# Feed-forward combinations joined to 1024 columns, and the scale of the up values on ScalarE

## The chip, the cores and the metric

The kernel runs on one core of a Trainium2 chip. The metric is the device time of one execution in microseconds (us), the median of three runs. Five engines work in parallel, each through its own list of instructions in a fixed order: TensorE (PE, with its weight loads shown apart as PEld), VectorE (DVE), ScalarE (ACT), GpSimd (POOL) and SyncE (SP), which issues most of the transfers. An instruction that has to wait holds back all that stands behind it on its engine.

## The reference

Two layers work on 256 positions of 2048 features in float32. Each layer is a mixer (first a gated delta rule beside a linear recurrence, then two kinds of attention) and a feed-forward part. Only the feed-forward part is touched here:

```python
def swiglu(hn, w_gate, w_up, w_down):
    return (jax.nn.silu(hn @ w_gate) * (hn @ w_up)) @ w_down
...
        h = h + swiglu(rmsnorm(h, ffn_norm[layer]), ffn_w_gate[layer], ffn_w_up[layer], ffn_w_down[layer])
    return rmsnorm(h, final_norm)
```

The inner width is 5632. `h` is the residual. The factor 1/rms of the norm is not applied to the input of the products but to their results, one number for each position (`nrm["rs"]`).

## The kernel before

**Products in three parts.** A float32 product is made of three products of a shorter float type. Each weight tile `raw` (128 partitions x 1024 columns) is loaded by SP, rounded by ACT to `whi` (L179), and the rest `wlo = raw - whi` is made by DVE (L180). PE then does high x high, high x low and low x high (L409, L410, L411), 512 columns each. Four buffers hold `whi`, three hold `wlo`. So each weight tile costs one ACT and one DVE instruction of 1024 columns before PE can use it.

**Blocks.** In `ffn` the work comes in blocks. A gate block makes 512 columns of the gate product and 512 of the up product for two groups of 128 positions; a down block makes 1024 columns of the down product. A block sums in four PSUM banks `F[t][i]`: `t` is the group of positions and `i` gate or up (in a down block, the left or right half). There are 11 gate blocks and 6 down blocks in each of the two feed-forward parts, in three pieces of 4, 4 and 3 gate blocks, each with two down blocks behind it. All blocks but the first of each part take a share of their weights in Strassen's way, with seven products in place of eight: sums of weight tiles (`T`, L384, split into `thi` at L376 and `tlo` at L377) meet combinations of the inputs (`comb`, made in `combine`, L387 to L398), and the results go into four more banks `M[0]` to `M[3]`. The `acc` pool has four banks for `F`, the `msp` pool four for `M` and for the transposes.

**The sums over the banks.** When its seven products are done, `ends` (L460) joins the banks `M` into four tiles of 128x512 in SBUF, `e[t][i]`: an ACT copy of `M[0]` and four DVE additions or subtractions (L464), each with one bank as input. After the block a gate block adds `F` to each tile (L529 for gate, L533 for up), takes the SiLU of the gate on ACT with the scale by 1/rms (L530), and multiplies: one DVE `scalar_tensor_tensor` for each `t` that scales the up values and multiplies them by the gate (L534). A down block adds `h` to each of the four tiles (L554), and then the sum to `F`, which gives the new `h` (L561; L557 at the very end).

**What follows.** The result of a gate block is transposed by PE into two banks `Ph` (`turn`, L498) in the next block, copied by ACT (L507), and its low part is taken by DVE (L508). These are the inputs `hid` of the down blocks.

**The order.** The program is written in the order of the algorithm; a planner that works with costs of its own puts the instructions of each engine into their final order. Only the end of the last block on DVE and ACT is ordered by hand. Where an instruction becomes shorter or waits for something else, the planner can put its neighbours elsewhere too, on every engine.

Of the kernel before, what the change touches and what calls it, by code (L numbers as in the profile page):

```python
# [5 lines left out]
AF = mybir.ActivationFunctionType  # L6
# [41 lines left out]
def body(tc, A, out):  # L48
# [338 lines left out]
    def combine(x4):  # L387
# [6 lines left out]
        for i, (x, y) in enumerate(((a21, a22), (a21, a11), (a22, c[:, 1]), (a12, c[:, 2]))):  # L394
            V.tensor_tensor(out=c[:, i], in0=x, in1=y, op=ALU.subtract)
# [18 lines left out]
    def sums():  # L414

        return [[mx.tile([128, 512], F32, name=f"e{t}{i}", tag=f"e{t}{i}", bufs=1) for i in range(2)] for t in range(2)]

    def block(src, x, comb, nd, hooks, tail=0, lead=2, trail=None):
# [41 lines left out]
        def ends():  # L460
            (c1, w5), (v, w7) = sums()
            S.copy(c1, M[0].t)
            for o, a, b, op in ((v, M[2], c1, ALU.subtract), (w5, M[1], v, ALU.add), (v, M[3], v, ALU.add), (w7, M[3], w5, ALU.add)):
                V.tensor_tensor(out=o, in0=a.t, in1=b, op=op)  # L464
            return [[c1, w5], [v, w7]]
# [27 lines left out]
    def ffn(L, then, fin=None):  # L493
# [18 lines left out]
        for groups in ((0, 2, 2, 2), (2, 2, 2, 2), (2, 2, 2)):  # L512
            piece = len(groups)
            hid = ogp.tile([128, 16, 2, T], F32R, name="hid", tag="hid")
            late = {4: lambda hid=hid: ch.update({0: combine(hid[:, 0:4])})}
            for j in range(piece):
                hooks = {2: turn} if todo else {}
                if b == 0:
                    hooks[5] = lambda: cx.update({0: combine(X[:, 0:4])})
                    hooks[8] = rstd  # L520
                    hooks[10] = lambda: cx.update({1: combine(X[:, 4:8])})
                if j == 1 and piece == 3:

                    hooks[6] = late[4]
                F, e = block(lambda i, u: gu[b, u, i], lambda k: X[:, k], {m: lambda m=m: cx[m] for m in range(groups[j])}, 4, hooks)
                a = e or sums()
                for t in range(2):
                    if e:
                        V.tensor_tensor(out=a[t][0], in0=F[t][0], in1=e[t][0], op=(ALU.add, ALU.subtract)[t])  # L529
                    S.activation(a[t][0], a[t][0] if e else F[t][0], AF.Silu, scale=nrm["rs"][:, t:t + 1])  # L530
                for t in range(2):
                    if e:
                        V.tensor_tensor(out=a[t][1], in0=F[t][1], in1=e[t][1], op=ALU.add)  # L533
                    V.scalar_tensor_tensor(out=a[t][0], in0=a[t][1] if e else F[t][1], scalar=nrm["rs"][:, t:t + 1],  # L534
                                           in1=a[t][0], op0=ALU.mult, op1=ALU.mult)
                    todo.append((hid, j, t, a[t][0]))
                b += 1
            u0 = 2 * (b - piece)
            for p in range(2):
                end = b == NB and p == 1  # L540
                hooks = {2: turn} if todo else {}
                if p == 0 and piece == 4:
                    hooks.update(late)
# [754 lines left out]
```

## Time and profile before

| what | value |
|---|---|
| median of three runs | 2227.28 us (2226.58 to 2227.33) |
| the profiled execution's own time | 2228.4 us |
| its span | 2226.6 us |
| busy share of the span | PE 99%, PEld 83%, DVE 86%, ACT 58%, POOL 2% |
| mean granted clock of TensorE | 0.999 |
| first feed-forward part (first to last of its products) | 432.4 to 1127.9 us |
| second feed-forward part | 1524.5 to 2217.7 us |

In the rows of the profile, `out<-in` names the tiles, `xN` is a count, and what follows the bar is the busy time, the mean of one instruction in ns, and the idle time of the engine before them with what ended it. In the time-ordered view the first number is the start, the second the length. On DVE and ACT the recorded lengths of neighbours overlap by a little, so what one more instruction costs is read from start to start.

### The profile page before, as it was taken

The page shows a single profiled execution, that of the slowest core. Times are in us where ns is not written, and L with a number is a line of the kernel's source. Part 1 is how long each engine was busy: PE and PEld are TensorE (multiplying, and loading weights), DVE is VectorE, ACT ScalarE, POOL GpSimd, SP SyncE. Part 2 cuts the span into 40 slices and gives each one's busy share as a digit, 9 for nine tenths or more (in the row PEclk, how much of TensorE's full clock was granted, in tenths as well). Part 3 has the DMA queues.
Part 4 walks back from the last instruction along what each step waited for, and adds up shares of the span by engine and source line. Part 5 has one row for each costly group of instructions (what it writes and reads, how often), then busy time and mean ns, then how long its engine had stood idle before and what let it go on. Part 6 is the DMA issues. An engine that isn't in the chain of part 4 may idle for free.

```text
span 2226.6 us, 30372 instructions
## 1 busy us (share of the span) xinstructions
PE 2211.8 (99%) x11002; PEld 1847.0 (83%) x11002; DVE 1917.1 (86%) x2713; ACT 1284.9 (58%) x1687; POOL 50.6 (2%) x62
## 2 busy tenths in 40 slices
PE   9999999999999999999999999999999999999998
PEld 8888888888888888888878888888888888888886
DVE  8899676679999999999966658866999999999998
ACT  6776664555555665555654444545665566555565
POOL 0000000000000000000000000000000000000000
PEclk9999999999999999999999999999999999999999
DMA  7445445677777776777665455556777777777774
GB/s 281 155 146 163 141 152 184 208 223 227 212 227 231 220 233 211 225 230 225 193 196 171 161 169 175 168 178 185 223 226 216 221 225 238 219 214 239 218 236 151
DMA packets 125992, 451.67 MB, mean 203 GB/s; under 512 B 14065, under 2 KB 15601, under 8 KB 125713
## 3 DMA queue, kind: packets, MB, share of 16 engines
q1 hardware_dynamic: 117488, 420.10, 58.3%
q0 software_dynamic: 8064, 29.36, 7.8%
q8 instruction: 86, 1.41, 0.3%
q14 instruction: 66, 0.53, 0.1%
q10 hardware_dynamic: 288, 0.27, 0.0%
HBM read 447.58 MB, written 2.10 MB: 202 GB/s over the span
## 4 chain that ended last, share of the span: by engine, by line
PE 95%; DVE 2%; issue 1%; ACT 1%; DMA 1%; DVEq 0%; ACTq 0%
PE F L411 15%; PE F L410 15%; PE F L409 15%; PE Pw L199 10%; PE Pw L204 5%; PE Px L303 5%; PE Px L304 5%; PE Px L305 5%; PE M L410 5%; PE M L411 4%; PE M L409 4%; PE Ph L503 1%; DVE wlo L180 1%; PE Psc L1068 1%; PE Pt L326 0%
## 5 line engine op out<-in xcount | busy, mean ns | idle before, releaser
L179 ACT CAST whi<-raw 128x1024 fp32r<-128x1024 f32 x720 | 755.3, 1051 | 666.8 <-PE F L411 263.8
L180 DVE TENSOR_TENSOR wlo<-raw,whi 128x1024 fp32r<-128x1024 f32 x720 | 874.5, 1219 | 189.3 <-PE Px L304 70.1
L199 PE MATMUL Pw<-X,whi 128*128 128x512 f32 x1088 | 388.3, 400 | 0.0
L409 PE MATMUL F<-whi,X 128*128 128x512 f32 x848 | 331.4, 391 | 0.0
L410 PE MATMUL F<-wlo,X 128*128 128x512 f32 x848 | 330.4, 390 | 0.0
L411 PE MATMUL F<-whi,X 128*128 128x512 f32 x848 | 330.0, 389 | 0.0
L204 PE MATMUL Pw<-X,wlo 128*128 128x256 f32 x1088 | 304.8, 280 | 1.0 <-DVE wlo L180 0.9
L376 ACT CAST thi<-T 128x1024 fp32r<-128x1024 f32 x168 | 176.6, 1051 | 124.1 <-DVE T L384 84.0
L199 PEld LDWEIGHTS Pw<-X,whi 128*128 128x128 f32 x1088 | 204.2, 188 | 47.7 <-issue 0.5
L377 DVE TENSOR_TENSOR tlo<-T,thi 128x1024 fp32r<-128x1024 f32 x168 | 205.1, 1221 | 28.0 <-ACT thi L376 27.3
L204 PEld LDWEIGHTS Pw<-X,wlo 128*128 128x128 f32 x1088 | 205.3, 189 | 2.4 <-DVE wlo L180 2.0
L409 PE MATMUL F<-whi,hid 128*128 128x512 f32 x480 | 187.5, 391 | 0.0
L411 PE MATMUL F<-whi,hid 128*128 128x512 f32 x480 | 186.9, 389 | 0.0
L410 PE MATMUL F<-wlo,hid 128*128 128x512 f32 x480 | 186.8, 389 | 0.0
L411 PEld LDWEIGHTS F<-whi,X 128*128 128x128 f32 x848 | 159.2, 188 | 33.1
L409 PEld LDWEIGHTS F<-whi,X 128*128 128x128 f32 x848 | 159.2, 188 | 32.7
L410 PEld LDWEIGHTS F<-wlo,X 128*128 128x128 f32 x848 | 159.2, 188 | 32.4
L384 DVE TENSOR_TENSOR T<-T,raw 128x1024 f32<-128x1024 f32 x112 | 136.5, 1219 | 1.1 <-DMA raw<-in_gu 0.2
L410 PE MATMUL M<-tlo,comb 128*128 128x512 f32 x336 | 131.8, 392 | 1.1 <-DVE tlo L377 1.0
L409 PE MATMUL M<-thi,comb 128*128 128x512 f32 x336 | 131.4, 391 | 0.0
L411 PE MATMUL M<-thi,comb 128*128 128x512 f32 x336 | 130.9, 390 | 0.0
L411 PEld LDWEIGHTS F<-whi,hid 128*128 128x128 f32 x480 | 90.1, 188 | 18.8
(389 smaller groups left out, 3409.5 us busy)
## 6 DMA issues: line engine op xcount, KB each, us to landing
raw<-in_gu SPq DMA_DIRECT2D x352, 512.0 KB, 4.4
raw<-in_dn SPq DMA_DIRECT2D x176, 512.0 KB, 4.4
raw<-in_w0w SPq DMA_DIRECT2D x72, 512.0 KB, 3.6
raw<-in_wo SPq DMA_DIRECT2D x64, 512.0 KB, 3.6
raw<-in_w1w SPq DMA_DIRECT2D x64, 512.0 KB, 3.6
raw<-in_gu POOLq DMA_DIRECT2D x40, 512.0 KB, 6.8
raw<-in_w1x SPq DMA_DIRECT2D x32, 512.0 KB, 3.7
raw<-in_w0x SPq DMA_DIRECT2D x16, 512.0 KB, 3.6
```

The source lines that it names most:

```text
L179: S.copy(hi, raw)
L180: V.tensor_sub(lo, raw, hi.bitcast(F32))
L199: PE.matmul(P.rearrange("p a b -> p (a b)"), hi[:, kk], X[:, k].rearrange("p a b -> p (a b)"), start=k == 0, stop=False)
L204: PE.matmul(P[:, 0], lo[:, kk], X[:, k, 0], start=False, stop=k == NK - 1)
L303: PE.matmul(Ps[t], x[:, 0, ts], hi[:, kk], start=k == 0, stop=False)
L304: PE.matmul(Ps[t], x[:, 0, ts], lo[:, kk], start=False, stop=False)
L376: S.copy(hi, t)
L377: V.tensor_sub(lo, t, hi.bitcast(F32))
L384: V.tensor_tensor(out=t, in0=a, in1=b, op=ALU.add)
L409: PE.matmul(self.t, xh, hi[:, kk], start=self.i == kk == 0, stop=False)
L410: PE.matmul(self.t, xh, lo[:, kk], start=False, stop=False)
L411: PE.matmul(self.t, xl, hi[:, kk], start=False, stop=kk == 1 and self.i == self.n - 1)
```

## The change

Four edits:

1. In `combine` two of the four combinations of the inputs change their sign: the second is a11 - a21 (it was a21 - a11), the third a21 - a22 - a11 (it was the negative of that). The third is made from the first and no longer from the second. The count and the size of the instructions stay.
2. The four tiles `e[t][i]` become one tile `e` of 128x4x512. With the two signs turned, `ends` needs two DVE instructions of 512 columns and one of 1024 columns, which reads the bank `M[1]` twice and writes both up columns. This one needs `M[3]` to be done, and it is the last to read `M[1]`.
3. In a gate block the four additions of `F` stay. The up values are scaled by an ACT instruction each (L533, `Copy` with a scale), and one DVE multiplication of 1024 columns (L534) takes the place of the two of L534 before. It waits for all four ACT instructions.
4. In a down block `h` is added in two DVE instructions of 1024 columns (L553) and no longer in four of 512. The four additions of `F` (L561, L557) stay.

Two lambdas for the combinations of `hid` are also joined to one function, which moves nothing by itself. The line numbers of the changed kernel are used for it: L463, L464 and L465 are the three DVE instructions of `ends`, L532 is the addition of `F`.

```diff
-        for i, (x, y) in enumerate(((a21, a22), (a21, a11), (a22, c[:, 1]), (a12, c[:, 2]))):
-            V.tensor_tensor(out=c[:, i], in0=x, in1=y, op=ALU.subtract)
+        for i, x, y, op in ((0, a21, a22, ALU.subtract), (1, a11, a21, ALU.subtract), (2, c[:, 0], a11, ALU.subtract), (3, a12, c[:, 2], ALU.add)):
+            V.tensor_tensor(out=c[:, i], in0=x, in1=y, op=op)
...
-        return [[mx.tile([128, 512], F32, name=f"e{t}{i}", tag=f"e{t}{i}", bufs=1) for i in range(2)] for t in range(2)]
+        return mx.tile([128, 4, 512], F32, name="e", tag="e", bufs=1)
...
-            (c1, w5), (v, w7) = sums()
-            S.copy(c1, M[0].t)
-            for o, a, b, op in ((v, M[2], c1, ALU.subtract), (w5, M[1], v, ALU.add), (v, M[3], v, ALU.add), (w7, M[3], w5, ALU.add)):
-                V.tensor_tensor(out=o, in0=a.t, in1=b, op=op)
-            return [[c1, w5], [v, w7]]
+            e = sums()
+            S.copy(e[:, 0], M[0].t)
+            V.tensor_tensor(out=e[:, 1], in0=M[2].t, in1=e[:, 0], op=ALU.add)
+            V.tensor_tensor(out=e[:, 2], in0=M[3].t, in1=e[:, 1], op=ALU.add)
+            V.tensor_tensor(out=e[:, 1::2], in0=M[1].t.rearrange("p (a n) -> p a n", a=1).to_broadcast([128, 2, 512]),
+                            in1=e[:, 1:3], op=ALU.subtract)
+            return e
...
-                for t in range(2):
-                    if e:
-                        V.tensor_tensor(out=a[t][0], in0=F[t][0], in1=e[t][0], op=(ALU.add, ALU.subtract)[t])
-                    S.activation(a[t][0], a[t][0] if e else F[t][0], AF.Silu, scale=nrm["rs"][:, t:t + 1])
-                for t in range(2):
-                    if e:
-                        V.tensor_tensor(out=a[t][1], in0=F[t][1], in1=e[t][1], op=ALU.add)
-                    V.scalar_tensor_tensor(out=a[t][0], in0=a[t][1] if e else F[t][1], scalar=nrm["rs"][:, t:t + 1],
-                                           in1=a[t][0], op0=ALU.mult, op1=ALU.mult)
-                    todo.append((hid, j, t, a[t][0]))
+                for i, f in enumerate((AF.Silu, AF.Copy)):
+                    for t in range(2):
+                        if e is not None:
+                            V.tensor_tensor(out=a[:, 2 * t + i], in0=F[t][i], in1=a[:, 2 * t + i], op=ALU.add)
+                        S.activation(a[:, 2 * t + i], F[t][i] if e is None else a[:, 2 * t + i], f, scale=nrm["rs"][:, t:t + 1])
+                V.tensor_tensor(out=a[:, 0::2], in0=a[:, 1::2], in1=a[:, 0::2], op=ALU.mult)
+                for t in range(2):
+                    todo.append((hid, j, t, a[:, 2 * t]))
...
-                for t in range(2):
-                    for i in range(2):
-                        V.tensor_tensor(out=e[t][i], in0=hs[t][i], in1=e[t][i], op=ALU.subtract if t > i else ALU.add)
+                c = slice(2 * p * 512, (2 * p + 2) * 512)
+                for t in range(2):
+                    et = e[:, 2 * t:2 * t + 2].rearrange("p a n -> p (a n)")
+                    V.tensor_tensor(out=et, in0=h[:, t, c], in1=et, op=ALU.add)
```

Since the planner sets the order anew, instructions move. Three places matter to the prediction.

**DVE, from one gate block to the next** (the first Strassen block of the first part and the one behind it). `F` with its number is the old block's bank, `wlo<-raw_5347` in the first list and `wlo<-raw_5342` in the second belong to the new block's first weight tile, the `wlo` behind it to the second. Before:

```order
L180 TENSOR_TENSOR wlo<-raw,whi 128x1024
L529 TENSOR_TENSOR e_5250<-F_4972,e_5250 128x512
L384 TENSOR_TENSOR T<-T,raw 128x1024
L529 TENSOR_TENSOR e_5252<-F_4974,e_5252 128x512
L533 TENSOR_TENSOR e_5251<-F_4973,e_5251 128x512
L180 TENSOR_TENSOR wlo<-raw_5347,whi 128x1024
L534 SCALAR_TENSOR_TENSOR e_5250<-e_5251,rs,e_5250 128x512
L533 TENSOR_TENSOR e_5253<-F_4975,e_5253 128x512
L180 TENSOR_TENSOR wlo<-raw,whi 128x1024
L534 SCALAR_TENSOR_TENSOR e_5252<-e_5253,rs,e_5252 128x512
```

With the change:

```order
L180 TENSOR_TENSOR wlo<-raw,whi 128x1024
L532 TENSOR_TENSOR e<-F_4970,e 128x512
L180 TENSOR_TENSOR wlo<-raw_5342,whi 128x1024
L532 TENSOR_TENSOR e<-F_4972,e 128x512
L532 TENSOR_TENSOR e<-F_4971,e 128x512
L384 TENSOR_TENSOR T<-T,raw 128x1024
L532 TENSOR_TENSOR e<-F_4973,e 128x512
L180 TENSOR_TENSOR wlo<-raw,whi 128x1024 x2
L534 TENSOR_TENSOR e<-e 128x2x512
```

The second `wlo` of the new block stands behind the fourth addition of `F` in both lists. The sum of weights `T` has moved from before the second addition to just ahead of the fourth, and the multiplication, once two instructions among the `wlo`, now comes as one behind two of them.

**DVE, from a down block to the gate block behind it** (from the first piece to the second). `F_6378` and `F_6380` before, `F_6361` and `F_6363` with the change, are the banks that PE finishes last. Before:

```order
L554 TENSOR_TENSOR e_6644<-h,e_6644 128x512
L180 TENSOR_TENSOR wlo<-raw_6721,whi 128x1024
L561 TENSOR_TENSOR h<-F_6377,e_6641 128x512
L180 TENSOR_TENSOR wlo<-raw,whi 128x1024
L561 TENSOR_TENSOR h<-F_6379,e_6643 128x512
L561 TENSOR_TENSOR h<-F_6378,e_6642 128x512
L384 TENSOR_TENSOR T<-raw_6757,raw 128x1024
L561 TENSOR_TENSOR h<-F_6380,e_6644 128x512
L180 TENSOR_TENSOR wlo<-raw_6757,whi 128x1024
```

With the change:

```order
L465 TENSOR_TENSOR e<-M_6365,e 128x2x512
L377 TENSOR_TENSOR tlo<-T,thi 128x1024
L553 TENSOR_TENSOR e<-h,e 128x1024 x2
L561 TENSOR_TENSOR h<-F_6360,e 128x512
L561 TENSOR_TENSOR h<-F_6362,e 128x512
L561 TENSOR_TENSOR h<-F_6361,e 128x512
L180 TENSOR_TENSOR wlo<-raw_6698,whi 128x1024
L561 TENSOR_TENSOR h<-F_6363,e 128x512
L180 TENSOR_TENSOR wlo<-raw,whi 128x1024
```

The first `wlo` of the new gate block (`raw_6721` before, `raw_6698` now) has moved from ahead of the first addition of `F` to behind the third.

**PE, the same place.** The first products of the new gate block. Before:

```order
L409 MATMUL F_6713<-whi,X 128x512
L410 MATMUL F_6713<-wlo,X 128x512
L411 MATMUL F_6713<-whi,X 128x512
L409 MATMUL F_6713<-whi,X 128x512
L410 MATMUL F_6713<-wlo,X 128x512
```

With the change:

```order
L409 MATMUL F_6690<-whi,X 128x512
L409 MATMUL F_6692<-whi,X 128x512
L409 MATMUL F_6691<-whi,X 128x512
L409 MATMUL M_6694<-whi,X 128x512
L409 MATMUL M_6695<-thi,comb 128x512
L410 MATMUL F_6690<-wlo,X 128x512
```

Five products that need no low part are drawn ahead of the first that does. This happens at four places, at the first gate block of the second and third piece of each part. The same drawing ahead, by one or two products, stood at more places before, around `M[3]`.

More of the change, by code (lines that the diff above doesn't have):

```diff
@@ L514, in ffn @@
             hid = ogp.tile([128, 16, 2, T], F32R, name="hid", tag="hid")
-            late = {4: lambda hid=hid: ch.update({0: combine(hid[:, 0:4])})}
+            chs = lambda m, hid=hid: lambda: ch.update({m: combine(hid[:, 4 * m:4 * m + 4])})
             for j in range(piece):
@@ L542, in ffn @@
                 if p == 0 and piece == 4:
-                    hooks.update(late)
-                    hooks[9] = lambda hid=hid: ch.update({1: combine(hid[:, 4:8])})
+                    hooks.update({4: chs(0), 9: chs(1)})
                 if end and fin:
@@ L549, in ffn @@
                 F, e = block(lambda i, u: dn[2 * p + i, u0 + u], lambda k: hid[:, k],
-                             {m: lambda m=m: ch[m] for m in range(1 + (p == 1 and piece == 4))}, piece, hooks, *last)
+                             {m: lambda m=m: ch[m] for m in range(2 if p == 1 and piece == 4 else 1)}, piece, hooks, *last)
+                c = slice(2 * p * 512, (2 * p + 2) * 512)
+                for t in range(2):
+                    et = e[:, 2 * t:2 * t + 2].rearrange("p a n -> p (a n)")
+                    V.tensor_tensor(out=et, in0=h[:, t, c], in1=et, op=ALU.add)
                 hs = [[h[:, t, (2 * p + i) * 512:(2 * p + i + 1) * 512] for i in range(2)] for t in range(2)]
-                for t in range(2):
-                    for i in range(2):
-                        V.tensor_tensor(out=e[t][i], in0=hs[t][i], in1=e[t][i], op=ALU.subtract if t > i else ALU.add)
                 if end and fin:
                     with tc.manual_schedule(engines={V.engine, S.engine}):
-                        fin(lambda t, i: V.tensor_tensor(out=hs[t][i], in0=F[t][i], in1=e[t][i], op=ALU.add))
+                        fin(lambda t, i: V.tensor_tensor(out=hs[t][i], in0=F[t][i], in1=e[:, 2 * t + i], op=ALU.add))
                     continue
@@ L560, in ffn @@
                     for i in range(2):
-                        V.tensor_tensor(out=hs[t][i], in0=F[t][i], in1=e[t][i], op=ALU.add)
+                        V.tensor_tensor(out=hs[t][i], in0=F[t][i], in1=e[:, 2 * t + i], op=ALU.add)
                 if b == NB and not fin:
```

4 lines of the change are left out of this document (2 added, 2 removed).

## The prediction

> **What bounds the kernel now.** I read the page first, its busy line and its chain of waits:
>
> ```profile
> PE 2211.8 (99%) x11002; PEld 1847.0 (83%) x11002; DVE 1917.1 (86%) x2713; ACT 1284.9 (58%) x1687; POOL 50.6 (2%) x62
> PE 95%; DVE 2%; issue 1%; ACT 1%; DMA 1%; DVEq 0%; ACTq 0%
> ```
>
> PE is the chain, and DVE is the only other engine near its limit. The change touches the two feed-forward parts alone, so their stretches come next (columns: length, then busy time and count of PE, PEld, DVE, ACT, POOL, then clock, DMA share and GB/s):
>
> ```profile
> 432.40:1127.90 695.50, 694.66 (x3113) 573.15 (x3112) 652.97 (x698) 408.59 (x454) 24.32 (x28) 1.00 0.74 221
> 1524.50:2217.70 693.20, 692.89 (x3097) 571.44 (x3096) 646.90 (x691) 404.79 (x440) 24.17 (x28) 1.00 0.73 217
> 2217.70:2226.60 8.90, 0.18 (x1) 0.00 (x0) 4.11 (x10) 3.02 (x7) 0.00 (x0) 0.80 0.63 236
> ```
>
> A busy PE need not be a PE at full pace, since the products overlap. So I measure the pace from the starts. Between these two rows lie 56 steps of 512 columns each, none missing:
>
> ```profile
> 999.17 0.39 PE L410 MATMUL F<-wlo,X 128*128 128x512 f32 x1
> 1011.86 0.39 PE L409 MATMUL M<-thi,comb 128*128 128x512 f32 x1
> 2121.94 0.87 PE Ph L503 x8
> ```
>
> 12.69 / 56 = 0.2266 us for one product; a group of eight short transposes takes 0.87 us. The second part holds 3097 PE instructions, 96 of them short (88 of `Ph`, 8 of the norm): 3001 x 0.2266 + 12 x 0.87 = 690.4 us, of 693.2. The first holds 112 short ones: 680.0 + 14 x 0.87 = 692.2, of 695.5. So at full pace the two parts would be 2.8 + 3.3 = **6.1 us** shorter. That is the ceiling for anything that DVE or ACT can give back there. The waits by name say what part of it is real waiting (us in total, times, longest):
>
> ```profile
> PEld M L410 <- DVE tlo L377: 4.0, 8, 1.2
> PEld F L410 <- DVE tlo L377: 1.2, 6, 0.2
> ACT whi L179 <- PE F L411: 263.8, 217, 4.5
> ```
>
> 5.2 us in 14 places, all for a `tlo` of DVE. The rest is put down to no wait. The longest place:
>
> ```profile
> 968.62 0.39 PE L409 MATMUL F<-whi,X 128*128 128x512 f32 x1
> 969.77 0.50 PE L410 MATMUL M<-tlo,comb 128*128 128x512 f32 x1 [0.76 <-DVE tlo L377]
> 968.50 1.21 DVE L377 TENSOR_TENSOR tlo<-raw,thi 128x1024 fp32r<-128x1024 f32 x1
> ```
>
> PE has 969.77 - 968.62 - 0.23 = 0.9 us of waiting here, for a `tlo` that started at 968.50.
>
> **The change part by part.** The groups that it touches, and the 1024-column addition that stands for the new ones:
>
> ```profile
> L464 DVE TENSOR_TENSOR e<-M,e 128x512 f32<-128x512 f32 x128 | 84.9, 684 | 2.5 <-PE M L411 1.9
> L554 DVE TENSOR_TENSOR e<-h,e 128x512 f32<-128x512 f32 x48 | 31.2, 682 | 0.0
> L534 DVE SCALAR_TENSOR_TENSOR e<-e,rs,e 128x512 f32<-128x512 f32 x40 | 29.6, 745 | 0.0
> L384 DVE TENSOR_TENSOR T<-T,raw 128x1024 f32<-128x1024 f32 x112 | 136.5, 1219 | 1.1 <-DMA raw<-in_gu 0.2
> L530 ACT ACTIVATE e<-e,rs 128x512 f32<-128x512 f32 x40 | 28.5, 721 | 17.8 <-DVE e L529 17.1
> ```
>
> The recorded lengths overlap, so the price is read from start to start, in DVE's rows from a down block to the gate block behind it:
>
> ```profile
> 678.26 0.68 DVE L554 TENSOR_TENSOR e<-h,e 128x512 f32<-128x512 f32 x1
> 678.86 1.28 DVE L464 TENSOR_TENSOR e<-M,e 128x512 f32<-128x512 f32 x2
> 680.06 1.88 DVE L554 TENSOR_TENSOR e<-h,e 128x512 f32<-128x512 f32 x3
> 681.87 1.21 DVE L180 TENSOR_TENSOR wlo<-raw,whi 128x1024 fp32r<-128x1024 f32 x1
> 683.00 0.68 DVE L561 TENSOR_TENSOR h<-F,e 128x512 f32<-128x512 f32 x1
> 683.81 1.23 DVE L180 TENSOR_TENSOR wlo<-raw,whi 128x1024 fp32r<-128x1024 f32 x1
> 684.96 1.28 DVE L561 TENSOR_TENSOR h<-F,e 128x512 f32<-128x512 f32 x2
> 686.15 1.21 DVE L384 TENSOR_TENSOR T<-raw,raw 128x1024 f32<-128x1024 f32 x1
> ```
>
> 512 columns: (681.87 - 680.06) / 3 = 0.60 us. 1024 columns: 683.00 - 681.87 = 1.13 us. Joining two saves 1.20 - 1.13 = 0.07 us. The scaled multiplication is read at 519.24 and 519.90 in the fence below: 0.66 us.
>
> - `ends`, 32 blocks: 4 x 0.60 becomes 2 x 0.60 + 1.13, 32 x 0.07 = 2.2 us off DVE. The new operation reads one bank twice; no row shows that form. Its bounds are 1.13 (L384) and 1.20 us (two of L464); I take 1.13, since L464 and L554 cost alike with and without a bank.
> - The residual, 12 blocks: 12 x 2 x 0.07 = 1.7 us off.
> - The multiplication, 22 gate blocks: 2 x 0.66 becomes 1.13, 22 x 0.19 = 4.2 us off. The two blocks without Strassen's products are among them.
> - The signs in `combine`: as many instructions of the same size, no time.
> - ACT: 44 more instructions like L530, 44 x 0.72 = 31.7 us. ACT idles 286.9 + 288.4 = 575 us in the two parts, most of it because `whi` has no free buffer (the 263.8 us above). Cover enough; without it the price would be the 31.7.
> - Transfers: as many, of the same size.
>
> DVE: -8.1 us of 1300, 0.25 us a block. It lies beside PE, so it reaches the end only through the waits for `tlo`. By the 14 places, each shorter by no more than 0.25, that is 3.5 us at most, and nothing where the weights came late. I take **-1.0**, bounds 0 and -5.2.
>
> [...]
>
> **The waits that move.** First the down-to-gate places. PE's rows there:
>
> ```profile
> 684.92 0.39 PE L411 MATMUL F<-whi,hid 128*128 128x512 f32 x1
> 686.50 0.39 PE L409 MATMUL F<-whi,X 128*128 128x512 f32 x1
> ```
>
> The gate block begins at 686.50. Its first `wlo` was ready at 683.08 (681.87 + 1.21), 3.6 us ahead of its use. Now it stands behind the third addition of `F`. Laid on the same times: from 678.26 come `T` 1.13, 0.60, 1.13, `tlo` 1.13, 2 x 1.13 and two additions 1.20, which is 685.7; less the 0.6 that the first row of `ends` no longer takes ahead of it, 685.1. The third bank is done at 684.92 + 0.39 = 685.3. So the addition starts between 685.3 and 685.7, the `wlo` 0.60 later, and is ready between 687.1 and 687.5. PE, with five products drawn ahead, wants it at 686.50 + 5 x 0.227 = 687.6. It fits, by 0.1 to 0.5 us where it was 3.6. Bounds over the four places: 0 and 4 x 1.9 = 7.6 us (if it came behind the fourth addition as well, with its bank at 686.7 and 0.6 + 1.2 us behind that, and the next one late too). I take 4 x 0.1 = **+0.4**. A full bank is freed in time: the third by 686.3, PE wants it at 686.96.
>
> Second, the gate-to-gate places. The block of these rows begins at 518.66:
>
> ```profile
> 518.66 0.39 PE L409 MATMUL F<-whi,X 128*128 128x512 f32 x1
> 525.69 0.39 PE L410 MATMUL M<-tlo,comb 128*128 128x512 f32 x1
> 519.24 0.75 DVE L534 SCALAR_TENSOR_TENSOR e<-e,rs,e 128x512 f32<-128x512 f32 x1
> 519.90 0.69 DVE L533 TENSOR_TENSOR e<-F,e 128x512 f32<-128x512 f32 x1
> 520.51 1.22 DVE L180 TENSOR_TENSOR wlo<-raw,whi 128x1024 fp32r<-128x1024 f32 x1
> 521.64 0.75 DVE L534 SCALAR_TENSOR_TENSOR e<-e,rs,e 128x512 f32<-128x512 f32 x1
> 523.44 1.22 DVE L377 TENSOR_TENSOR tlo<-T,thi 128x1024 fp32r<-128x1024 f32 x1
> ```
>
> `tlo` was ready at 524.66 and wanted at 525.69, 1.0 us. Now: fourth addition done 1.0 us after the block's begin, two `wlo` to 3.3, the multiplication (ACT's last scale is done by 1.0 + one cast 1.05 + 0.72 = 2.8), so `tlo` from 4.4 to 5.7, wanted at 7.03: 1.3 us. Where the planner sets the multiplication one `T` behind the addition, DVE reaches it at 2.1 and waits up to 0.7 for ACT; behind it stand a `wlo` and that `tlo`, ready at 2.8 + 3 x 1.13 + 0.1 = 6.3, 0.7 us ahead. No time taken, bound in the rivals. The end of the kernel, 8.9 us, keeps its instructions.
>
> Sum: 2226.6 - 1.0 + 0.4 = 2226.0 for the span; the profiled execution with 1.8 us around it was 2228.4 against a median of 2227.28, so the median becomes 2226.7: **2226.7 us, no change that can be told.** Under 0.2% (4.5 us) I call no change, about what can be told apart here.
>
> **The rivals.**
>
> *A new wait for ACT (slower).* The multiplication in DVE's list waits for four ACT instructions. If ACT comes one cast of 1.05 us later than I have it, the 0.7 us is gone and each of the 22 gate blocks pays 0.35 us: 7.7 us, 2227.3 + 7.7 = 2235.0. For it: ACT and DVE are both bound in order, and SiLU already waits 17.1 us for DVE. Against it: ACT idles 41% here. It decides from 0.7 us of lateness. The 7.6 us of the down-to-gate places would look alike in the time. 0.14.
>
> *All waits for `tlo` go (faster).* -5.2 us: 2222.1. For it: every one ends with DVE. Against it: 0.25 us a block is less than the longest needs, 0.9. 0.08.
>
> *DVE is the bound (faster).* If PE were only seemingly full, each microsecond off DVE would count: -8.1 us, 2219.2. Against it: the 690.4 of 693.2 us. [...] 0.02.
>
> *The edit changes DVE's count but the planner gives the gain back by its new order, wait for wait*: 2227.3, inside my forecast.
>
> **How the numbers follow.** Forecast 0.76, from 2223.5 to 2230. The rivals 0.14, 0.08, 0.02. The slower one and the bounds of the four places reach up, so the range goes to 2232.0, half way into that rival; below to 2222.8, short of the faster ones. Faster by over 0.2% (below 2222.8): half of the 0.08, the 0.02 and 0.01 of the forecast, 0.07. Slower (above 2231.7): 0.12 of the 0.14 and 0.01, 0.13. Same: 0.80.
>
> **What would show it.** DVE should count 78 instructions less (32 + 24 + 22), and lose some 8 us of starts or 14 us of recorded lengths, ACT gain 44 instructions and 31 us; L465 and L553 should have near 1.22 us each. PE's two parts should stay within 3 us of 695.5 and 693.2. The waits `PEld M L410 <- DVE tlo` should stand at 3 to 4 us, and a wait for `wlo` of less than 2 us in all may appear at four places. I am wrong if DVE waits for L533 by tens of us in the list of waits, or if PE waits by over 1 us at the start of the pieces.

## The result, and the profile after

| | before | changed |
|---|---|---|
| median | 2226.93 us (2224.32 to 2227.33, 4 runs) | 2250.06 us (2244.14 to 2254.66, 4 runs) |
| ratio, with 95% interval | | 1.0105 (1.0093 to 1.0117) |
| profiled execution | 2228.4 us, span 2226.6 | 2244.1 us, span 2242.4 |

The changed kernel is slower by 1.05%, 23 us. I had forecast 2226.7 us and no change; the time lies far above the range. The profiled execution of the changed kernel is the shortest of its four, so its trace shows 15.8 us of the loss.

The page's busy line and the shares of the chain of waits, changed kernel:

```profile
PE 2218.5 (99%) x11002; PEld 1847.8 (82%) x11002; DVE 1909.0 (85%) x2635; ACT 1317.0 (59%) x1731; POOL 50.6 (2%) x62
PE 94%; DVE 2%; DMA 1%; issue 1%; ACT 1%; DVEq 0%; ACTq 0%
```

DVE has 78 instructions and 8.1 us less (1917.1 to 1909.0), ACT 44 instructions and 32.1 us more, both as forecast. The busy shares move by a point, and DMA appears in the chain no more than before. Nothing on this page says where 16 us went. The two feed-forward parts do (the columns are those of the prediction's second view):

```profile
431.12:1135.29 704.17, 698.71 (x3113) 573.95 (x3111) 648.18 (x658) 424.07 (x476) 24.35 (x28) 1.00 0.72 218
1531.97:2233.24 701.27, 695.56 (x3096) 571.20 (x3095) 642.84 (x652) 420.12 (x462) 24.18 (x28) 1.00 0.71 215
2233.40:2242.40 9.00, 0.23 (x2) 0.00 (x0) 4.10 (x10) 3.08 (x7) 0.00 (x0) 0.70 0.63 233
```

704.17 for 695.50 and 701.27 for 693.20: 8.7 + 8.1 = 16.8 us, the whole loss of this trace and 1 us more, since the rest of the kernel is that much shorter; the end takes 9.0 us for 8.9. The joined instructions themselves cost what was assumed (the groups, with the mean ns of one behind the busy time):

```profile
L465 DVE TENSOR_TENSOR e<-M,e 128x1024 f32<-128x1024 f32 x32 | 39.1, 1223 | 0.8
L553 DVE TENSOR_TENSOR e<-h,e 128x1024 f32<-128x1024 f32 x24 | 28.4, 1219 | 0.1
L534 DVE TENSOR_TENSOR e<-e 128x1024 f32<-128x1024 f32 x22 | 26.8, 1219 | 0.0
```

So the loss is new waiting of PE. The waits of PE and of its weight loads for `thi` and `tlo` in the changed kernel (total us, times, longest):

```profile
PEld M L409 <- ACT thi L376: 9.3, 10, 1.9
PEld M L410 <- DVE tlo L377: 8.7, 13, 1.1
PE M L409 <- ACT thi L376: 5.4, 5, 1.5
PE M L410 <- DVE tlo L377: 4.6, 6, 0.8
```

Before, the first of these was 1.0 us in 4, the second 4.0 in 8, the fourth 1.0 in 2, and the third did not exist. A stall can be in two of these rows, once for the weight load and once for the product, so they are not added up. Set beside each other product by product, the starts of PE in the two traces drift apart at few places. The largest are four, by 2.8, 4.5, 2.8 and 2.1 us, near 662, 916, 1763 and 2018 us: **12.2 of the 15.8 us**. Then come two, by 1.2 and 1.7 us, near 493 and 1594 us, in the first block of each part that uses Strassen's products. The four are all the same place of the program: the second down block of a piece of four gate blocks, the only blocks in a down product that take two of their weight blocks (seven products each) in Strassen's way.

**One of the four.** PE in the changed kernel at 662 us:

```profile
662.10 0.39 PE L411 MATMUL F<-thi,hid 128*128 128x512 f32 x1
663.96 0.50 PE L409 MATMUL M<-thi,comb 128*128 128x512 f32 x1 [1.47 <-ACT thi L376]
665.22 0.50 PE L410 MATMUL M<-tlo,comb 128*128 128x512 f32 x1 [0.76 <-DVE tlo L377]
```

Starts 1.86 and 1.26 us apart in place of 0.23: 2.7 us. The product that waits is the seventh of the first weight block, `M[3]`, whose `thi` ACT makes from `raw`. ACT there:

```profile
658.71 1.06 ACT L376 CAST thi<-T 128x1024 fp32r<-128x1024 f32 x1 [2.02 <-DVE T L384]
661.91 1.05 ACT L179 CAST whi<-raw 128x1024 fp32r<-128x1024 f32 x1 [2.14 <-DMA raw<-in_dn]
662.86 1.04 ACT L376 CAST thi<-raw 128x1024 fp32r<-128x1024 f32 x1
```

ACT is not busy, it waits: first for a sum `T` of DVE, then, until 661.91, for a transfer, and the `thi` that PE wants stands behind both. The load that ended the second wait was issued by SP at 655.30, 0.63 us behind a transfer of POOL. That one adds more weights to the tile that the first sum of a weight block has read, and POOL issues it only behind this sum (the adding transfer, from here on). The two issues, then for the load alone who waited for it, its time from issue to landing, and what SP had waited for:

```profile
654.67 0.86 POOL L443 DMA_DIRECT2D raw<-in_dn  x1 [16.49 <-DVE T L384]
655.30 0.33 SPq L173 DMA_DIRECT2D raw<-in_dn  x1
...
  ACT whi L179: 2.1, 1
DMA to landing us min/median/max: 6.5/6.5/6.5
...
SPq L173 <- DVE wlo L180: 3.6, 1, 3.6
```

So the load took 6.5 us, and it could not go out before a `wlo` of DVE had freed a buffer. DVE in the same place:

```profile
650.02 1.22 DVE L180 TENSOR_TENSOR wlo<-raw,whi 128x1024 fp32r<-128x1024 f32 x1
652.91 1.23 DVE L384 TENSOR_TENSOR T<-raw,raw 128x1024 f32<-128x1024 f32 x1 [1.67 <-DMA raw<-in_dn]
654.06 1.22 DVE L180 TENSOR_TENSOR wlo<-raw,whi 128x1024 fp32r<-128x1024 f32 x1
```

The row at 652.91 is the first sum of the *second* weight block. It waits 1.67 us for its own tile to land and holds back everything behind it. The `wlo` at 654.06 is the one that frees the buffer; it ends at 655.28, and SP issues at 655.30. The kernel before in the same place, DVE, then the same load in SP's list with its time to landing, then POOL and ACT:

```profile
651.78 2.35 DVE L180 TENSOR_TENSOR wlo<-raw,whi 128x1024 fp32r<-128x1024 f32 x2
654.05 1.22 DVE L384 TENSOR_TENSOR T<-T,raw 128x1024 f32<-128x1024 f32 x1
655.18 1.22 DVE L384 TENSOR_TENSOR T<-raw,raw 128x1024 f32<-128x1024 f32 x1
...
653.07 0.33 SPq L173 DMA_DIRECT2D raw<-in_dn  x1
DMA to landing us min/median/max: 3.4/3.4/3.4
...
656.93 0.86 POOL L443 DMA_DIRECT2D raw<-in_dn  x1 [15.03 <-ACT thi L376]
659.52 1.05 ACT L376 CAST thi<-raw 128x1024 fp32r<-128x1024 f32 x1 [0.30 <-PE M L411]
```

There the first sum of the second weight block stood two `wlo` and the third sum of the first weight block later, at 655.18, where its tile had landed and it waited for nothing. The load went out at 653.07, behind the first of these `wlo`, and landed 3.4 us later; the adding transfer went out behind it and behind the next load too. `thi` was made at 659.52 and PE took it at 662.00 with no stall. In the changed kernel the planner has moved this one sum ahead of two `wlo` and of the third sum. The load that PE's product hangs on is issued 2.2 us later (653.07 to 655.30) and takes 3.1 us longer (3.4 to 6.5), with the adding transfer now ahead of it. DVE's waits for a transfer ahead of `T`, in all (changed kernel; before there was the `in_gu` row alone, with 7.2 us in 8):

```profile
DVE T L384 <- DMA raw<-in_dn: 14.5, 13, 2.1
DVE T L384 <- DMA raw<-in_gu: 14.1, 12, 2.3
```

28.6 us of DVE's idle time for 7.2. DVE saved 8.1 us of work, and spent 21 us more in waiting for tiles. How much of that waiting costs PE anything is another matter, which after_pinned answers below.

### The profile page after: what moved, and what is told of

Read it like the earlier page. It is cut to its first block, busy times and chain, and to the rows that moved or that the text cites. A ratio compares the mean times of both kernels' runs of the same rounds, so it can differ in the third digit from the quotient of the medians.

```text
span 2242.4 us, 30326 instructions
## 1 busy us (share of the span) xinstructions
PE 2218.5 (99%) x11002; PEld 1847.8 (82%) x11002; DVE 1909.0 (85%) x2635; ACT 1317.0 (59%) x1731; POOL 50.6 (2%) x62
## 4 chain that ended last, share of the span: by engine, by line
PE 94%; DVE 2%; DMA 1%; issue 1%; ACT 1%; DVEq 0%; ACTq 0%
PE F L410 15%; PE F L409 15%; PE F L411 15%; PE Pw L199 11%; PE Pw L204 5%; PE Px L303 5%; PE Px L305 5%; PE Px L304 5%; PE M L410 4%; PE M L411 4%; PE M L409 4%; PE Ph L505 1%; DVE wlo L180 1%; DMA raw<-in_gu 1%; DMA raw<-in_dn 1%
## 5 line engine op out<-in xcount | busy, mean ns | idle before, releaser
L410 PE MATMUL F<-wlo,X 128*128 128x512 f32 x848 | 330.5, 390 | 0.0
L410 PE MATMUL F<-wlo,hid 128*128 128x512 f32 x480 | 187.1, 390 | 0.0
L410 PEld LDWEIGHTS F<-wlo,X 128*128 128x128 f32 x848 | 159.3, 188 | 32.5
L410 PE MATMUL M<-tlo,comb 128*128 128x512 f32 x336 | 132.6, 395 | 4.7 <-DVE tlo L377 4.6
```

The source lines that it names most:

```text
L410: PE.matmul(self.t, xh, lo[:, kk], start=False, stop=False)
```

## The experiments

The theory (A): the joins let DVE's order change, the first sum `T` of a second weight block comes ahead of data that has not landed, DVE stands still, buffers of `raw` come free late, loads go out and land late, and PE stalls some 10 us later. Its rivals: (B) the 44 more instructions on ACT make the casts late; (C) with the new signs bank `M[1]` is read behind the last product, `M[3]`, so banks come free late; (D) what the join in `ends` costs lies in that reading of `M[1]`; (E) `T` may not be late either; (F) in one place, the row of additions itself. In the table the place of `T` is counted in `wlo` of DVE's list against the kernel before, for the second weight block of the four down blocks, and of the first Strassen gate block of each part.

| run | T, down | T, first gate | median us | ratio to before (95%) |
|---|---|---|---|---|
| signs_only | 0 | 0 | 2232.97 | 1.0024 (1.0013 to 1.0035) |
| gate_only | 0 | -1 | 2234.09 | 1.0034 (1.0023 to 1.0046) |
| no_ends_join | 0 | -1 | 2233.97 | 1.0032 (1.0022 to 1.0042) |
| ends_only | -2 | 0 | 2239.37 | 1.0056 (1.0041 to 1.0071) |
| the change | -2 | -1 | 2250.06 | 1.0105 (1.0093 to 1.0117) |
| after_pinned | 0 | -1 | 2232.62 | 1.0025 (1.0015 to 1.0036) |
| ends_on_m3 | -2 | 0 | 2240.69 | 1.0064 (1.0049 to 1.0079) |
| ends_on_m3_pinned | 0 | 0 | 2228.37 | 1.0009 (0.9999 to 1.0018) |
| joins_old_signs_held | 0 | -1 | 2231.90 | 1.0020 (1.0011 to 1.0029) |
| signs_last_held | 0 | 0 | 2229.69 | 1.0013 (1.0004 to 1.0023) |
| after_all_held | +1 | -1 | 2236.51 | 1.0039 (1.0024 to 1.0054) |
| before_T_late | +2 | +3 | 2242.38 | 1.0069 (1.0054 to 1.0084) |
| after_T_late | +2 | +3 | 2243.66 | 1.0078 (1.0063 to 1.0093) |

All kernels with -2 in the first column lose 12.6 us or more against the one before; none with 0 loses more than 8. In the three with -2, at all four places, DVE waits 1.2 to 2.1 us for the tile ahead of `T`, the adding transfer goes out two loads sooner than in the kernel before, and the load right behind it takes 6.4 to 7.4 us from issue to landing. The same load takes 3.4 to 4.6 us in the kernel before, after_pinned and ends_on_m3_pinned, where DVE waits for nothing there.

An early sum is not enough by itself. In ten of the thirteen kernels the first sum in the gate block behind each of these down blocks is two `wlo` early as well; its tile has landed there, DVE waits for nothing, SP's next load comes 2.5 us or more behind the adding transfer, and PE keeps its pace (no start more than 0.24 us behind the last).

### Which part of the change

**signs_only** takes the three joins out of the changed kernel again:

```diff
-            V.tensor_tensor(out=e[:, 1::2], in0=M[1].t.rearrange("p (a n) -> p a n", a=1).to_broadcast([128, 2, 512]),
-                            in1=e[:, 1:3], op=ALU.subtract)
+            V.tensor_tensor(out=e[:, 3], in0=M[1].t, in1=e[:, 2], op=ALU.subtract)
+            V.tensor_tensor(out=e[:, 1], in0=M[1].t, in1=e[:, 1], op=ALU.subtract)
...
-                    V.tensor_tensor(out=et, in0=h[:, t, c], in1=et, op=ALU.add)
+                    for i in range(2):
+                        V.tensor_tensor(out=e[:, 2 * t + i], in0=hs[t][i], in1=e[:, 2 * t + i], op=ALU.add)
...
-                V.tensor_tensor(out=a[:, 0::2], in0=a[:, 1::2], in1=a[:, 0::2], op=ALU.mult)
+                    V.scalar_tensor_tensor(out=a[:, 2 * t], in0=F[t][1] if e is None else a[:, 2 * t + 1], scalar=nrm["rs"][:, t:t + 1],
+                                           in1=a[:, 2 * t], op0=ALU.mult, op1=ALU.mult)
```

> The changed kernel with its new signs and the joint tile e, but with all three joins undone: ends, residual and multiplication run in pieces of 512 columns, the scale of the up values stays on DVE. Theory A (DVE's order: in the down block with two Strassen weight blocks the sum T of the second one stands ahead of casts' rests wlo that free the raw tiles, and DVE waits there for a transfer): here that T stands where it stood before, so 2227 us, within 2 us of the kernel before, and PE does not stall by 3 us at the four places near 662, 916, 1763 and 2018 us. Theory B (ACT has more to do, 44 instructions, and its casts come late): no new ACT work here, 2227 us. Theory C (with the new signs bank M1 is read behind the last product M3, so banks come free late): the signs are all here, so 2235 to 2245 us.

Measured: 2232.97 us, +6.2 against 2226.79 of the same round. The four stalls are not there. But no theory had +6 here; the trace has most of it in one place, near 2186 us, which comes below.

**ends_only** adds the join in `ends` to that, the first two lines above undone.

> As the run with the signs alone, plus the join of the two sums over bank M1 in ends to 1024 columns; residual and multiplication in pieces of 512. Theory A: this join moves T of the second weight block two rests wlo ahead in the four down blocks with two weight blocks; DVE waits about 1.7 us for its transfer and PE stalls by 2.7 us or more at each of the four places: 2227 + 4 x 2.7 = 2238 us, 2236 to 2242. Theory B: no new ACT work, 2227 us. Theory C: as the run with the signs alone.

Measured: 2239.37 us, +12.6. The four stalls are there, by 2.9, 1.7, 2.1 and 4.2 us, with the one near 2186 us gone. 10.9 us of stalls, less 4.9 of that place, is 6.0, and the medians differ by 6.4.

**gate_only** adds the scale of the up values on ScalarE and the joined multiplication to signs_only, the last lines above undone.

> As the run with the signs alone, plus the scale of the up values on ScalarE and the multiplication in 1024 columns; ends and residual in pieces of 512. Theory A: T of the second weight block stays in its place in the down blocks, but in the first gate block of each part it stands one rest wlo ahead: two stalls of about 1.2 us, 2229 to 2230 us, and no stalls at 662, 916, 1763 and 2018 us. Theory B: all the 44 ACT instructions are here, so all or nearly all of the loss: 2240 to 2250 us. Theory C: as the run with the signs alone.

Measured: 2234.09 us, 1.1 above signs_only: that is all, on balance, that 44 more ACT instructions and DVE's new wait for them cost, and B falls. A's 2229 to 2230 us did not have the 6 us of the signs in it. The stalls near 488 and 1584 us are there, by 0.9 and 1.1 us, as the moved `T` said.

**no_ends_join** is the whole change with the two `M[1]` lines of 512 columns put back.

> The whole change without the join in ends: bank M1 is read twice by two instructions of 512 columns, everything else as changed (signs, residual and multiplication in 1024 columns, 44 more instructions on ACT). Theory A: T of the second weight block in the down blocks with two stands where it stood before, so the four stalls are gone; what is left is that of the run with the signs and the multiplication, 2234 us, 2232 to 2236. If ACT's 31.7 us more or the residual's join cost something of their own: over 2238 us.

Measured: 2233.97 us, as gate_only. So the residual's join costs nothing that can be told, and the join in `ends` carries 16 us of the 23 in the whole change. Beside the signs alone it was 6.4: the parts do not add up.

### Whether it is T's place

**after_pinned** is the whole change with one edge more in DVE's order, from the third sum of the first weight block to the first sum of the second; it adds no instruction and no data that has to be waited for:

```diff
-        V.tensor_tensor(out=t, in0=a, in1=b, op=ALU.add)
+        if behind:
+            with tc.issue_after(behind[0]):
+                i = V.tensor_tensor(out=t, in0=a, in1=b, op=ALU.add)
+        else:
+            i = V.tensor_tensor(out=t, in0=a, in1=b, op=ALU.add)
+        third[:] = [i.ins]
...
-            t, w = total(b11, b12)
+            t, w = total(b11, b12, behind=third[:] if m > min(comb) else ())
```

> The whole change, and one thing more: the sum T of the second weight block is held in DVE's order behind the third sum of the first weight block, where it stood before. No instruction is added or taken away. Theory A: the four places lose their stalls (4 x 2.7 us by the gaps between PE's starts, up to 4 x 4.5 us with the slower clock behind them): 2228 to 2234 us; what is left is the first gate block of each part and smaller waits. Theories B and C: nothing changes, 2244 to 2255 us.

Measured: 2232.62 us, 17.4 below the change. The wait lists of PE and DVE in this run (lines past 380 stand 7 lower; L388 is the held sum, L390 all others):

```profile
PE M L416 <- ACT thi L376: 1.4, 3, 0.7
DVE T L388 <- DMA raw<-in_gu: 4.5, 2, 2.3
DVE T L390 <- DMA raw<-in_dn: 7.9, 9, 1.5
DVE T L390 <- DMA raw<-in_gu: 9.5, 9, 1.9
```

PE's waits for `thi` fall from 5.4 to 1.4 us. The two waits of a held `T` that remain are those of the first gate blocks, where it is still one `wlo` early; PE loses 1.9 and 2.0 us there. What counts is where DVE waits, not the sum of all its waits for tiles. The hold takes away the four of the down blocks, 6.9 us, and with them the 12.2 us of stalls of PE; 20 others are still there, 21.9 us (three of the rows above, L388 and L390). Those near 606 and 638 us, 2.0 us together, cost PE nothing that its starts show.

**ends_on_m3** settles C and D. It is the kernel before with its old signs, and one join only, of the two sums over `M[3]`, which need no new sign if the four tiles lie in the order v, w7, c1, w5:

```diff
-            for o, a, b, op in ((v, M[2], c1, ALU.subtract), (w5, M[1], v, ALU.add), (v, M[3], v, ALU.add), (w7, M[3], w5, ALU.add)):
-                V.tensor_tensor(out=o, in0=a.t, in1=b, op=op)
+            V.tensor_tensor(out=v, in0=M[2].t, in1=c1, op=ALU.subtract)
+            V.tensor_tensor(out=w5, in0=M[1].t, in1=v, op=ALU.add)
+            V.tensor_tensor(out=e[:, 0:2], in0=M[3].t.rearrange("p (a n) -> p a n", a=1).to_broadcast([128, 2, 512]),
+                            in1=e[:, 0::3], op=ALU.add)
```

> The kernel before with all its signs, the tile e in one piece, and one join alone: the two sums over bank M3 in ends in 1024 columns, M3 + (v, w5), in place of two of 512. M1 is read early, as before; residual, multiplication and scales as before. DVE has 1.13 us behind the last product in place of 1.20. Theory A (T of the second weight block in the down blocks with two comes two rests wlo ahead, and DVE waits there for its transfer): T stands two rests ahead here too, so the four stalls come back without any new sign: 2226.8 + 10.9 (the four places of the run with the join in ends: 2.9 + 1.7 + 2.1 + 4.2) = 2237.7, 2234 to 2241 us. Theory D (what the join in ends costs comes from bank M1 being read and freed behind the last product): 2225 to 2229 us.

Measured: 2240.69 us, +14.2, with 32 instructions and some 2 us of work less on DVE, and `M[1]` read as early as ever. C and D fall as causes of the four stalls. DVE and PE in this run at the first of the four places:

```profile
651.37 1.23 DVE L384 TENSOR_TENSOR T<-raw,raw 128x1024 f32<-128x1024 f32 x1 [1.42 <-DMA raw<-in_dn]
...
662.54 0.50 PE L409 MATMUL M<-thi,comb 128*128 128x512 f32 x1 [0.24 <-ACT thi L376]
663.80 0.50 PE L410 MATMUL M<-tlo,comb 128*128 128x512 f32 x1 [0.76 <-DVE tlo L377]
```

Here they came by 1.4, 1.3, 2.4 and 1.3 us, 6.4 in all and less than the 10.9 expected; two others, by 1.9 and 1.6 us, came in the gate blocks behind (715 and 1816 us), where `T` stands one `wlo` early.

**ends_on_m3_pinned** is the same with the edge of after_pinned.

> As the run with the sums over M3 joined, and T of the second weight block held in DVE's order behind the third sum of the first one. Theory A: the four stalls go, 2226 to 2229 us, the kernel before or a little under it (the joins take 32 x 0.07 = 2.2 us off DVE, beside PE). Theory D: no difference to the run without the hold.

Measured: 2228.37 us, 12.3 below its twin, and with the kernel before within what can be told. The same sum in the same place, and the row of PE's list that is left:

```profile
653.79 1.22 DVE L387 TENSOR_TENSOR T<-raw,raw 128x1024 f32<-128x1024 f32 x1
...
PE M L413 <- DVE tlo L377: 0.6, 2, 0.3
```

It waits for nothing now. Two kernels with the same instructions on every engine, and with the same order on PE, SP and POOL, differ by 12 us through the place of one sum in DVE's list and what the planner moves with it: a third sum in the gate block behind, and on ACT one cast `thi` in either place. Between the change and after_pinned it is the held sum, also in one more block of each part, and the cast. So A holds in this: the place of the sum makes the four stalls. How much of a stall comes from DVE's wait and how much from the adding transfer, which goes out early with the sum, no run separates.

### Whether later is better

**before_T_late** and **after_T_late** hold the first sum of every weight block behind the `wlo` of its own first tile:

```diff
-        V.tensor_sub(lo, raw, hi.bitcast(F32))
+        rest[:] = [V.tensor_sub(lo, raw, hi.bitcast(F32)).ins]
...
-        V.tensor_tensor(out=t, in0=a, in1=b, op=ALU.add)
+        with tc.issue_after(rest[0]) if own else ExitStack():
+            V.tensor_tensor(out=t, in0=a, in1=b, op=ALU.add)
```

> The kernel before with the same hold: T behind the rest wlo of its own first tile. Its DVE waits for raw ahead of T are 7.2 us in 8. Theory A in its narrow form: 2224 to 2227 us. Theory E: stalls at the last products, over 2232 us.

> The whole change, with T of every weight block held in DVE's order behind the rest wlo of its own first tile, which puts it 0 to 5 rests (1.13 us each) behind its place in the kernel before. DVE should no longer wait for a transfer ahead of T (28.6 us in 25 waits in the changed kernel, under 5 here). Theory A in its narrow form (only DVE's wait ahead of T counts): the four stalls go and those of the first gate blocks too, 2227 to 2232 us. Theory E (T must not be late either, since the accumulating transfer starts behind it and needs 6.6 us until the last product of the weight block wants its tile): stalls come back at the last products, over 2240 us.

Measured: 2242.38 and 2243.66 us. DVE's list of waits has no row for a transfer ahead of `T` any more, and both kernels are 16 and 17 us slower than the one before. So DVE's wait is not the cost by itself; E holds. The weight loads of PE in before_T_late:

```profile
PEld M L412 <- ACT thi L378: 14.8, 44, 0.7
PEld F L412 <- ACT thi L378: 7.9, 15, 1.7
```

59 waits for `thi` in place of four of 0.3 us or less: many short ones, as many as there are weight blocks (56) and a few more. 38 of them, 12.6 of the 22.7 us, are for the `thi` of the tile that POOL's transfer adds to. Whether the sums themselves are late there or the transfer that adds to the tile (issued by POOL behind the first sum) is open. `T` has a window: two `wlo` early in four blocks costs 12 us, up to five late in all blocks costs 16.

### What the signs cost

In signs_only PE stalls near 2186 us, in the last piece. Windows there (from and to, length, then busy time and count of PE, PEld, DVE, ACT, POOL, clock, DMA share, GB/s):

```profile
2184.00:2188.00 4.00, 2.86 (x13) 2.05 (x11) 4.00 (x7) 2.00 (x2) 0.00 (x0) 1.00 0.83 210
2188.00:2191.00 3.00, 2.36 (x7) 1.23 (x8) 3.00 (x6) 2.78 (x7) 0.00 (x0) 0.98 0.03 8
2191.00:2194.00 3.00, 3.00 (x9) 2.33 (x8) 2.32 (x3) 0.95 (x3) 0.00 (x0) 0.50 0.75 195
```

DVE is full, and the transfers have all but stopped (share 0.03): in DVE's list the second sum and eight additions follow on each other without a `wlo` that would free a buffer. **signs_last_held** holds the first sum of the last down block behind the residual additions of the block before:

```diff
+                        if b == NB and p == 0 and 2 * t + i == 3:
+                            mark[:] = [r.ins]
...
-            t, w = total(b11, b12)
+            t, w = total(b11, b12, hold=mark)
```

> The run with the signs alone (2233 us), with T of the last down block held in DVE's order behind the four residual additions of the block before it. In the signs alone PE loses 4.9 us at one place, 2172 to 2196 us, where T, the second sum and eight additions stand ahead of one rest wlo. Theory A (T's place makes this stall too): the place loses its stall, 2227 to 2230 us. Theory F (the row of additions itself, which the new signs put behind the last product M3, makes it): still 2231 us or more.

Measured: 2229.69 us, 3.3 below signs_only. The same stretch now:

```profile
2184.00:2188.00 4.00, 4.00 (x19) 3.34 (x18) 3.96 (x6) 1.25 (x2) 0.00 (x0) 1.00 0.38 141
2188.00:2191.00 3.00, 3.00 (x15) 2.46 (x14) 3.00 (x4) 2.58 (x6) 0.00 (x0) 1.00 0.36 83
2191.00:2194.00 3.00, 3.00 (x15) 2.49 (x14) 3.00 (x4) 3.00 (x5) 0.86 (x1) 1.00 0.73 198
```

F's time did not come: with `T` held, the stall is gone. That the place of `T` alone made it is not shown. The hold moved the second sum and a `tlo` back as well, the planner set `wlo` between the additions of `F`, and PE's order changed at this place. Some 3 us of the signs remain, in places of 0.4 to 0.7 us each, and are not settled.

### Whether the joins are worth something without the stalls

**joins_old_signs_held** takes ends_on_m3_pinned, adds the joined multiplication with the scale on ScalarE, and joins the residual where the old signs allow it:

```diff
+                V.tensor_tensor(out=w4[:, 0::2], in0=w4[:, 1::2], in1=w4[:, 0::2], op=ALU.mult)
...
+                et = w4[:, 2:4].rearrange("p a n -> p (a n)")
+                V.tensor_tensor(out=et, in0=h[:, 0, 2 * p * 512:(2 * p + 2) * 512], in1=et, op=ALU.add)
```

> The kernel before with its signs, and the joins as far as these signs allow: the sums over M3 in ends, the multiplication with the scale of the up values on ScalarE, the residual of the first row half (the second half has two signs and stays in 512 columns); T of the second weight block held behind the third sum of the first one. DVE has 2.2 + 4.2 + 0.8 = 7.2 us of work less than before by starts. Theory A: no stalls at the four places; T stands one rest early in the first gate blocks and some others, which cost 2 us in the run with the multiplication: 2228 to 2231 us. If DVE's work set the time: 2226.5 - 7.2 = 2219 us.

Measured: 2231.90 us, just above what A allowed. DVE was 1909.5 us busy in place of 1917.1, and the time rose: some 1.1 us at each of three gate blocks (near 496, 1589 and 2092 us), where `T` is one `wlo` early, and smaller ones. DVE's work does not set the time.

**after_all_held** is the whole change with the first sum of both weight blocks held, behind the third sum, the residual additions, or the last additions to `h`:

```diff
+            third[:] = [V.tensor_tensor(out=t, in0=a, in1=b, op=ALU.add).ins]
...
-            t, w = total(b11, b12)
+            t, w = total(b11, b12, hold=third[:])
...
+                    third[:] = [V.tensor_tensor(out=et, in0=h[:, t, c], in1=et, op=ALU.add).ins]
...
+                        if p:
+                            third[:] = [i_.ins]
```

> The whole change, with T of the second weight block held behind the third sum of the first, and T of the first weight block held behind the residual additions (second down block) or the last additions to h (gate block behind it). T then stands 0 or one rest behind its place in the kernel before in the down blocks, one rest ahead in the first gate blocks as without the hold. Theory A: as the run with the second T alone held (2232.6 us) or better, 2227 to 2233 us. Theory E (late T): where one rest is too late, over 2235 us.

Measured: 2236.51 us, 3.9 above after_pinned, in which only the second one is held, and outside A's range. Whether the lateness of one `wlo` already costs something is not shown: the intervals of the two ratios overlap, and of the two executions with a trace this one is the shorter (2233.88 against 2236.77 us). No version beat the kernel before.

## Why the prediction was wrong

**What bounds the kernel** was right: PE at full pace, with 6.1 us to be had. Not all of the waits by name were for a `tlo`: the list of the kernel before also has 1.0 us in 4 for a `thi` of ACT and 1.0 us in 4 for `hid`. With so little to win, a change beside PE can do more harm than good, and I drew that conclusion for the gain alone.

**DVE's saving** was right in every term: 78 instructions, 8.1 us, 1223 and 1219 ns for the joined ones, and 32.1 us more on ACT beside idle time. The new operation that reads one bank twice took 1223 ns, as the one without a bank, 1219. In recorded length a join of two additions of 512 columns saves 2 x 684 - 1219 = 149 ns; the busy time, in which overlaps count once, fell by 8.1 us. The -1.0 us that I took from DVE's saving for the end did not come, and no run here shows it: with the stalls held away, the joins measured +1.9 us (ends_on_m3_pinned, with an interval that reaches just below nothing) and +5.4 (joins_old_signs_held).

**The step that failed** is that under "The waits that move". It looked for moved waits in two kinds of places, down to gate and gate to gate, and worked out where the `wlo` and `tlo` would stand there. It left out the third kind, from the first down block to the second, where two weight blocks in Strassen's way follow each other; and in all of them it laid `T` into DVE's list by length alone ("from 678.26 come `T` 1.13, ..."), as if its tile had landed. With it went the line "Transfers: as many, of the same size", a term put at nothing: right in number and size, but a transfer also has a time of issue, here the time at which DVE frees a buffer or finishes a sum, and a place among the others. The runs put in its place: the join in `ends` moves the first sum of the second weight block two `wlo` ahead, and it waits 1.7 us for its tile. The load that PE's product hangs on goes out 2.2 us later, now behind the adding transfer, and lands 6.5 us after its issue in place of 3.4. PE stalls 2.1 to 2.8 us at three of the four places, and 4.5 us at the one where its clock falls to 0.50, some 1.6 of them by the clock. Held back, 17.4 of the 23 us are gone.

**The down-to-gate places**, +0.4 by my sum with a bound of 7.6: PE's lists have no wait for a `wlo` in the feed-forward parts, so the margin held. **The gate-to-gate places**: 2.9 us in the two first gate blocks, where I had no time. They come in the kernels whose `T` is one `wlo` early there and in no other; these two were not held alone.

**The rivals.** *A new wait for ACT* was the slower one, with a place and a price; gate_only shows 1.1 us for the whole edit, and the joined multiplication had 0.0 us of idle time ahead of it. My slower side had the right sign and the wrong mechanism. *All waits for `tlo` go* and *DVE is the bound* fall with joins_old_signs_held. *The planner gives the gain back* is what happened, only not "wait for wait": a new order is not bounded by the gain that set it off. That is why the range was far too narrow at its top: 7.7 us was the worst that I had priced, and the waits that one moved sum can make in four blocks are more than that.

**What would show it.** The PE parts should have stayed within 3 us; they grew by 8.7 and 8.1. `PEld M L410 <- DVE tlo` stands at 8.7 us in place of 3 to 4. Both of my signs of being wrong (DVE waiting for L533, PE waiting at the start of the pieces) stayed away; the stall was in the middle of a block.

## What to carry to other kernels

Where a planner sets the order and PE is full, an edit that only makes another engine's work shorter has little to give and can still cost much (here 6.1 us at most, and 23 lost): look in the new order for instructions that read a freshly loaded tile and have moved ahead, and set their new time against the landing of the load, not against the engine's own list. Here DVE waited 1.67 us at the head of its list, which delayed the `wlo` that freed a load buffer, and the bill came one load later, on PE, some 10 us on. Look also at the transfers that a moved instruction sets off: here one of them went out ahead of two loads that were wanted sooner. A moved instruction can be tested by holding it in its old place with an ordering edge and nothing else; here that gave back 17 of 23 us, while holding the first sums of all weight blocks far back cost 16 us.

## What the runs showed of the hardware

**One stall cost more than its length.** At 916 us PE stalls as at 662 us, and then runs at a lower clock (windows of the changed kernel):

```profile
912.58:916.00 3.42, 3.42 (x16) 2.70 (x15) 3.42 (x4) 1.25 (x2) 0.00 (x0) 1.00 1.02 319
916.00:919.41 3.41, 1.24 (x4) 0.49 (x4) 1.68 (x3) 3.41 (x4) 0.00 (x0) 1.00 0.87 281
919.41:922.82 3.41, 3.41 (x9) 2.64 (x9) 3.15 (x3) 0.41 (x2) 0.00 (x0) 0.50 0.56 197
922.82:926.24 3.42, 3.42 (x16) 2.80 (x15) 1.56 (x2) 1.99 (x2) 0.00 (x0) 1.00 0.45 163
```

The granted clock is 0.50 for 3.41 us. Products start 0.43 us apart in place of 0.227: eight steps take 3.39 us in place of 1.81, so some 1.6 us more are lost. The stalls at 662 and 1763 us, as long, left the clock at 1.00. In signs_only the clock is at 0.50 too, from about 2190.9 us (0.98 and then 0.50 in its last two rows above). The clock's changes in the traces of the two kernels lie whole multiples of 3.4133 us apart. In the changed kernel the first is at 8.05 us, where products of 256 columns go from 0.21 to 0.12 us from start to start; 919.41 lies 267 of these steps behind it, and 922.82 one more. In the kernel before, 649 steps lie between the changes at 7.75 and 2223.00 us. Counted in these steps, the stall at 916 us leaves one, 916.00 to 919.41, in which only three products start, 1.80 and 1.26 us apart. Those at 662, 1763 and 2018 us fall across two steps, with six or more starts in each. The number of starts does not settle it: in signs_only PE has seven products in the 3.00 us of the row in which the clock falls. What sets off such a spell, no run shows. The four executions of the changed kernel have mean clocks of 0.998, 0.996, 0.997 and 0.996 for 2244.1, 2254.7, 2249.7 and 2250.4 us, and after_pinned 0.998 to 0.999: by the rows above one spell lowers the mean by 0.0008 and costs 1.6 us, so the three longer executions would have one to three spells more. That is an estimate of 2 to 4 us of the 5.6 to 10.5 by which they are longer; only the shortest execution has a trace, and the rest stays open.

**Loads close behind an adding transfer landed late.** At the four places the kernel before has such a load 0.63 us behind POOL's transfer, both of 512 KB. From issue to landing it takes 7.6, 8.0, 9.0 and 6.9 us, and the two loads just ahead of the transfer take 3.4 to 4.2. There no cast waits for it; in the changed kernel it is the load that PE's product hangs on.
